# Scaling behind the SwiGLU's output products instead of ahead of them, in a fused encoder block on one Trainium2 core

## The chip, the core and the metric

The kernel runs on one core of one Trainium2 chip. The core has a matrix engine (TensorE, PE in the profile, with its weight loads as PEld), a vector engine (DVE), a scalar engine (ACT), GpSimd (POOL, hardly used here), and a sync engine (SP) whose queue issues the loads and stores. The metric is the device time of one execution in microseconds, as the median of three runs.

## What is computed

One encoder layer on 1024 tokens of 1024 channels in fp32: a half-weighted SwiGLU feed-forward (FFN1), a token mixer (retention with four heads beside a multi-scale pooling branch, both gated), a second half-weighted SwiGLU (FFN2), and a last norm. What bears on the change:

```python
D_MODEL = 1024; SEQ = 1024; D_FF = 2816; FFN_RES_WEIGHT = 0.5

def rmsnorm(x, g):
    y = x * lax.rsqrt(jnp.mean(x * x, axis=-1, keepdims=True) + NORM_EPS)
    return y * g

def swiglu_ffn(x, w_in, w_out):
    gate, up = jnp.split(x @ w_in, 2, axis=-1)
    return (jax.nn.silu(gate) * up) @ w_out

h = h + FFN_RES_WEIGHT * swiglu_ffn(rmsnorm(h, norm_ffn1), ffn1_w_in, ffn1_w_out)
...
h = h + merged @ w_out
h = h + FFN_RES_WEIGHT * swiglu_ffn(rmsnorm(h, norm_ffn2), ffn2_w_in, ffn2_w_out)
return rmsnorm(h, norm_final)
```

The norm's factor of a token is one number for each token. In the kernel it is not applied to the input of the first product but to its results: `(x g) @ w_in` is computed on unnormalised rows, and gate and up are multiplied by the factor afterwards. `silu(r·gate) · (r·up) @ w_out` equals `r · (silu(r·gate) · up) @ w_out`, since r belongs to the token.

## The kernel before

Activations lie with channels on the partitions and tokens along the free dimension, so that the factor of all tokens is a row, spread over 128 partitions into one 128x1024 tile `rb`. Each fp32 product is made as three products of rounded parts: `split` (L153 to L155) copies a value's rounded part on ACT (`hi`) and subtracts it on DVE (`lo`, L155); `mm3` (L172 to L176) issues the three matmuls on lines 174, 175 and 176. Large products are Strassen products of 512x512 blocks.

The order of the work comes from two places. `Flow` (L57 to L87) runs a chain of steps, each a pair of a preparation and a body: preparations (loads, sums, splits of weights) are issued four steps (`LOOK`) ahead of the bodies (the matmuls and their evacuations). Work that isn't urgent goes into a queue by `flow.add`, and one or two items of it are issued behind each body (`flow.rate`); `flow.until` issues such items until a condition holds. The framework then orders the instructions of each engine when it builds the program, with what stands under `soon()` (high priority) ahead of the rest. Every engine runs its instructions in that order. Tiles come from pools with fixed numbers of buffers: `mv` 28, `t4` 9, `raw` 4, `wt` 5, `tl` 4, `c2` 8 (128x512), and PSUM banks.

`ffn_in` (L699 to L769) makes the 22 groups of 128 gate channels and 128 up channels, each as a gate tile and an up tile of 128x1024. Its groups run in pairs (`pairs_of_both`, with `strassen`, L421, and `common`, L527 to L583, which shares the products of two groups in a common bank `x` that L569 and L580 evacuate). `evac` (L713 to L722) brings each 512-wide quarter of gate or up out of PSUM: where the factor is there and the quarter comes straight from one bank, L718 multiplies it on the way; otherwise it is copied or added, and a multiplication with the factor (L722) is queued. `end` queues the Silu (L728), two 512-wide products gate x up (L731), and for every second group the sums that the output stage's Strassen operands need (L744, L745, L749, L754), which are stored to DRAM (`R`, `T`, `B`, `T4`). In FFN1 the products begin before the factor is known; the groups finished by then wait with their multiplications. Names with `a_` and `n1` are FFN1's, those with `c_` and `n3` FFN2's.

`ffn_out` (L801 to L987) runs the seven Strassen products p1 to p7 over 11 steps `k` each, p1 alternating with p6, then p2 with p7, then p5, p3, p4. Its accumulators `acc` are eight 128x1024 tiles which are loaded with the residual (`res`: x, or h2 from DRAM) at `k == 6` of p1 (L829 to L832). As each product's banks end, `onto` (L891 to L896) adds half of the bank to a quarter (L894), and `after1` (L898 to L908) adds p1's halved bank, kept as `h`, to three quarters (L902, L906). When a quarter is complete it goes to `sink` through the queue: in FFN1 the next norm's quarters and a store, in FFN2 the last norm's sums of squares. In FFN2 the last product p4 is made with its operands exchanged (`near`, `far`), so that half of the tokens come out with tokens on the partitions: `split_scaled` (L157 to L159) halves the operand there, and class `Last` (L1667 to L1757) turns the accumulators for these tokens with transposes (`turned`, L1695 to L1707), finishes the rows (`finish`, L1719 to L1733), and makes the other half's norm (`end`, `fin0sum` at L223, L1754). Names with `b` (bacc, bp1a) are FFN1's output stage, those with `d` (dacc, dp4m, dL22a) FFN2's.

Of the kernel before, what the change touches and what calls it, by code (L numbers as in the profile page):

```python
# [17 lines left out]
P = 128  # L18
S = 1024
# [71 lines left out]
def block_kernel(ctx: ExitStack, tc, x, x_tok, vecs, f1_in, f1_out, w_in, w_v, pool_w, w_ret, w_pool, w_o,  # L91
# [16 lines left out]
    def mv(name):  # L108
        return sb.tile([P, 2, H], F32R, tag="mv", bufs=N_MV, name=name)
# [10 lines left out]
    def tl(name):  # L120
        return sb.tile([P, S], F32, tag="tl", bufs=N_TL, name=name)
# [4 lines left out]
    def c2(name):  # L126
        return sb.tile([P, H], F32, tag="c2", bufs=N_C2, name=name)
# [8 lines left out]
    def load(dst, src):  # L136
        nc.sync.dma_start(dst, src)
# [4 lines left out]
    def half(t, j):  # L142
        return t[:, j * H : (j + 1) * H]
# [9 lines left out]
    def split(hi, lo, src):  # L153
        copy(hi, src)
        tt(lo, src, hi.bitcast(F32), SUB)  # L155
# [5 lines left out]
    def operand(src, name):  # L161
        m = mv(name)
        split(m[:, 0], m[:, 1], src)
        return m
# [534 lines left out]
    def ffn_in(nx, w, ops, name, start=None):  # L699

        R, T, B, T4 = ops
        hid = {}

        def group(g):
            gate_up = {}

            def dest(which):
                tile, j = which
                if tile not in gate_up:
                    gate_up[tile] = (tl if start and g == 0 else t4)(f"{name}{'gu'[tile]}{g}")  # L710
                return half(gate_up[tile], j)

            def evac(which, in0, in1):  # L713
                j, dst = which[1], dest(which)
                if in1 is not None:
                    tt(dst, in0, in1, ADD)
                elif nx.rb is not None:
                    tt(dst, in0, half(nx.rb, j), MUL)  # L718
                    return
                else:  # L720
                    copy(dst, in0)
                flow.add(lambda: tt(dst, dst, half(nx.rms(), j), MUL))  # L722

            def end():
                gate, up = gate_up[0], gate_up[1]

                def swish():
                    act(gate, gate, AF.Silu)  # L728

                def times(j):  # L730
                    tt(half(up, j), half(gate, j), half(up, j), MUL)  # L731

                flow.add(swish, lambda: times(0), lambda: times(1))
                hid[g] = up
                k = g % FH
                if g < FH:
                    return
                lo, hi, e = hid.pop(k), up, {}
                R11, R12, R21, R22 = half(lo, 0), half(lo, 1), half(hi, 0), half(hi, 1)

                def w1():

                    e["n"], e["m"] = gate, c2(f"{name}m{k}")
                    tt(half(e["n"], 0), R12, R11, SUB)  # L744
                    tt(half(e["n"], 1), R22, R12, SUB)  # L745
                    load(B[k], e["n"])

                def w2():
                    tt(R12, R22, half(e["n"], 0), SUB)  # L749
                    load(R[k], lo)  # L750
                    load(T[k], hi)

                def w3():
                    tt(e["m"], R21, R12, SUB)  # L754
                    load(T4[k], e["m"])
                    done.add(k)

                flow.add(w1, w2, w3)

            if start and g == 0:  # L760
                return plain_group(nx, start, f"{name}{g}_", evac, end)
            return lambda shared: strassen(nx, w[g, 0], w[g, 1], f"{name}{g}_", evac, end, shared=shared, dest=dest)

        done = ops_done.setdefault(name, set())
        order = [g for k in range(FH) for g in (k, k + FH)]
        if start:

            return chain(group(0), pairs_of_both(nx, (group(g) for g in order[1:]), BY_OPERAND, 3))
        return pairs_of_both(nx, (group(g) for g in order), BY_OPERAND, 2)  # L769
# [28 lines left out]
    ops_done = {}  # L798


    def ffn_out(ops, ready, w, res, name, sink, end, last=None):  # L801

        R, T, B, T4 = ops
        t, acc = {}, {}
        S1, S2, S3 = {}, {}, {}

        def kept(store, n, k):
            if k % 2 == 0:  # L810
# [3 lines left out]
        def both(key, k, src):  # L814

            if k % 2 == 0:
                t[key] = (tl if key[0] != "L" else raw)(f"{name}{key}{k}")
                n = min(2, FH - k)
                for z in range(n):
                    load(half(t[key], z), src(k + z))  # L820
            return half(t[key], k % 2)

        def p1(k):
            flow.until(lambda: k in ready)
            r = tl(f"{name}r{k}")
            load(r, R[k])
            ra = raw(f"{name}ra{k}")
            load(ra, w[k, :, :S])
            if k == 6:  # L829
                for mt in range(KT):  # L830
                    acc[mt] = t4(f"{name}acc{mt}")
                    load(acc[mt], res[mt])  # L832
            t["x"] = half(ra, 0), half(ra, 1), both("L22a", k, lambda z: w[z, :, 2 * H : 3 * H])
            t["r"] = r
            return half(ra, 0), half(r, 0)
# [7 lines left out]
            return s2, half(t["r"], 1)  # L843

        def p2(k):
            r = tl(f"{name}q{k}")
            load(half(r, 0), T[k][:, :H])
            load(half(r, 1), B[k][:, H:])
            t["r"] = r
            L12, s2 = both("L12", k, lambda z: w[z, :, 3 * H :]), half(S2[k // 2], k % 2)  # L850

            tt(s2, L12, s2, SUB)
            return L12, half(r, 0)

        def p7(k):
            return half(S3[k // 2], k % 2), half(t["r"], 1)

        def p5(k):
            return half(S1[k // 2], k % 2), both("T1", k, lambda z: B[z][:, :H])

        def p3(k):
            return half(S2[k // 2], k % 2), both("R22", k, lambda z: T[z][:, H:])

        def p4(k):
            return both("L22", k, lambda z: w[z, :, 2 * H : 3 * H]), both("T4", k, lambda z: T4[z])

        bk = {}
# [20 lines left out]
        def quarter(mt, j):  # L888
            return half(acc[mt], j)

        def onto(mt, j, where, i, last=True):  # L891
            q = quarter(mt, j)
            with soon():
                stt(q, bk[where, i], 0.5, q, MUL, ADD)  # L894
            if last:
                flow.add(lambda: sink(mt, slice(j * H, (j + 1) * H), acc[mt]))  # L896

        def after1(i):  # L898
            h = c2(f"{name}p1{i}")
            with soon():  # L900
                act(h, bk["a", i], AF.Copy, scale=0.5)
                tt(quarter(i, 1), quarter(i, 1), h, ADD)  # L902

            def rest():
                for j in (1, 0):
                    tt(quarter(i + 4, j), quarter(i + 4, j), h, ADD)  # L906

            flow.add(rest)  # L908

        def after6(i):  # L910
            onto(i, 1, "b", i, False)

        def after2(i):
            onto(i, 0, "a", i)

        def after7(i):
            onto(i + 4, 1, "b", i, False)
            if last:

                onto(i + 4, 0, "b", i, False)  # L920
                if i == 3:
                    flow.add(*last.turned(acc))

        def after5(i):
            onto(i + 4, 1, "a", i)

        def after3(i):
            onto(i, 1, "a", i)
            if i == 3:
                end(0)  # L930

        def after4(i):
            onto(i + 4, 0, "b", i)
            if i == 3:
                end(1)

# [93 lines left out]
    def ffn1():  # L1030
        for n, step in enumerate(ffn_in(first, f1_in, ops1, "a", lead)):
            flow.rate = 1 if n < 40 else 2
            yield step
        yield from ffn_out(ops1, ops_done["a"], f1_out, x, "b", mix.quarter, end1)

    mix = Next("n2", V_MIX, h1)

# [727 lines left out]
    flow.run(chain(ffn1(), projections(), retention(), merge(), second(),  # L1765
                   ffn_out(ops2, ops_done.setdefault("c", set()), f2_out, h2, "d", fin.quarter, fin.end, fin)))
    flow.some(-1)


# [84 lines left out]
```

## Time and profile before

| | us |
|---|---|
| median of 3 runs | 2161.77 (2161.57 to 2161.9) |
| the profiled execution's own time | 2165.61 |
| span of that execution | 2163.8 |
| FFN1 input stage | 13 to 430 |
| FFN1 output stage | 430 to 675, the mixer's norm behind it |
| projections, retention, merge | 675 to 1540 |
| FFN2 input stage | 1540 to 1940 |
| FFN2 output stage | 1940 to 2125 |
| last products and final norm | 2125 to 2163.8 |

The profile is of one execution, whose own time is 3.8 us above the median. A row of a group of instructions reads: line, engine, operation, output <- inputs, count, durations in ns (least/median/most), first and last start, shapes. A row of the timeline reads: start, duration, engine, line, operation, and in brackets the idle time before it with what ended it. A row of the waits reads: engine, instruction, what it waited for, us in total, times, longest. Shown durations of instructions that follow each other on one engine overlap, so that a group's cost is its starts' distance, not its duration.

### The profile page before, as it was taken

How to read it: one execution, taken by the hardware profiler on the slowest of the kernel's cores; microseconds unless marked ns; L12 is line 12 of the kernel's file. 1: busy time of each engine (PE TensorE's matmuls, PEld its weight loads, DVE VectorE, ACT ScalarE, POOL GpSimd, SP SyncE). 2: the span in 40 equal slices, each digit the busy share in tenths (PEclk: the TensorE clock that was granted, in tenths of full speed). 3: DMA queues.
4: the chain of work that ended last, by engine and by line, in shares of the span. 5: the costliest groups of instructions: out<-in, count | busy, mean ns of one | idle time of the engine just before them, and what ended most of it. 6: DMA issues, size and time to landing. Idle time of an engine off the chain costs nothing.

```text
span 2163.8 us, 29697 instructions
## 1 busy us (share of the span) xinstructions
PE 2148.3 (99%) x10668; PEld 1816.2 (84%) x10668; DVE 1869.9 (86%) x3300; ACT 1088.1 (50%) x2047; POOL 0.2 (0%) x4
## 2 busy tenths in 40 slices
PE   9999999999999999999999999999999999999998
PEld 7888888888888888888888898888888888888887
DVE  8799899998778798899767877899999989999784
ACT  8544444545656444444426754446644444455463
POOL 0000000000000000000000000000000000000000
PEclk9999999999999999999999999999999999999999
DMA  7232323496323333333485567624132332359532
GB/s 255 75 118 99 115 93 124 159 337 211 127 93 98 117 127 108 115 110 116 154 268 192 166 227 255 220 92 161 64 120 100 106 104 93 117 183 336 177 122 78
DMA packets 117828, 320.92 MB, mean 148 GB/s; under 512 B 12976, under 2 KB 17200, under 8 KB 117680
## 3 DMA queue, kind: packets, MB, share of 16 engines
q1 hardware_dynamic: 117104, 317.97, 43.3%
q8 instruction: 83, 1.36, 0.3%
q10 hardware_dynamic: 576, 1.05, 0.1%
q14 instruction: 65, 0.53, 0.1%
HBM read 228.27 MB, written 90.70 MB: 147 GB/s over the span
## 4 chain that ended last, share of the span: by engine, by line
PE 89%; DVE 8%; DMA 1%; issue 1%; ACT 1%; SPq 0%; DVEq 0%; ACTq 0%
PE c_b L174 2%; PE c_b L176 2%; PE c_b L175 2%; PE c_e L176 2%; PE a_b L176 2%; PE a_b L174 2%; PE a_b L175 2%; PE c_e L175 2%; PE c_e L174 2%; PE a_e L176 1%; PE bp6b L176 1%; PE bp6b L175 1%; PE bp6b L174 1%; PE a_e L174 1%; PE a_e L175 1%; PE c_a L175 1%
## 5 line engine op out<-in xcount | busy, mean ns | idle before, releaser
L175 PE MATMUL c_b<-n3T,c_wS 128*128 128x512 f32 x176 | 68.5, 389 | 0.0
L176 PE MATMUL c_b<-n3T,c_wS 128*128 128x512 f32 x176 | 68.5, 389 | 0.0
L174 PE MATMUL c_b<-n3T,c_wS 128*128 128x512 f32 x176 | 68.3, 390 | 0.0
L174 PE MATMUL a_b<-n1T,a_wS 128*128 128x512 f32 x168 | 65.4, 389 | 0.0
L176 PE MATMUL a_b<-n1T,a_wS 128*128 128x512 f32 x168 | 65.4, 389 | 0.0
L175 PE MATMUL a_b<-n1T,a_wS 128*128 128x512 f32 x168 | 65.4, 389 | 0.0
L176 PE MATMUL a_a<-n1R,a_wL 128*128 128x512 f32 x120 | 47.0, 393 | 0.8 <-DVE a_wL L155 0.8
L175 PE MATMUL a_a<-n1R,a_wL 128*128 128x512 f32 x120 | 47.2, 393 | 0.0
L174 PE MATMUL a_a<-n1R,a_wL 128*128 128x512 f32 x120 | 47.1, 393 | 0.0
L175 PE MATMUL c_a<-n3R,c_wL 128*128 128x512 f32 x112 | 43.8, 391 | 0.0
L176 PE MATMUL c_a<-n3R,c_wL 128*128 128x512 f32 x112 | 43.7, 390 | 0.0
L174 PE MATMUL c_a<-n3R,c_wL 128*128 128x512 f32 x112 | 43.6, 389 | 0.0
L176 PEld LDWEIGHTS c_b<-n3T,c_wS 128*128 128x128 f32 x176 | 33.0, 188 | 6.9
L174 PEld LDWEIGHTS c_b<-n3T,c_wS 128*128 128x128 f32 x176 | 33.1, 188 | 6.8
L175 PEld LDWEIGHTS c_b<-n3T,c_wS 128*128 128x128 f32 x176 | 33.1, 188 | 6.8
L174 PEld LDWEIGHTS a_b<-n1T,a_wS 128*128 128x128 f32 x168 | 31.5, 188 | 6.7 <-ACT a_v L477 0.2
L175 PEld LDWEIGHTS a_b<-n1T,a_wS 128*128 128x128 f32 x168 | 31.5, 188 | 6.6
L176 PEld LDWEIGHTS a_b<-n1T,a_wS 128*128 128x128 f32 x168 | 31.5, 188 | 6.5
L176 PE MATMUL c_e<-n3T,c_wS 128*128 128x512 f32 x88 | 35.1, 399 | 0.5 <-DVE c_wS L155 0.4
L174 PE MATMUL c_e<-n3T,c_wS 128*128 128x512 f32 x88 | 34.4, 391 | 0.0
L176 PE MATMUL c_e<-n3T,c_wL 128*128 128x512 f32 x88 | 34.4, 391 | 0.0
L175 PE MATMUL c_e<-n3T,c_wL 128*128 128x512 f32 x88 | 34.4, 391 | 0.0
(3058 smaller groups left out, 8071.0 us busy)
## 6 DMA issues: line engine op xcount, KB each, us to landing
c_ra<-in_f_in SPq DMA_DIRECT2D x22, 512.0 KB, 3.6
c_rb<-in_f_in SPq DMA_DIRECT2D x22, 512.0 KB, 4.2
a_ra<-in_f_in SPq DMA_DIRECT2D x21, 512.0 KB, 3.6
a_rb<-in_f_in SPq DMA_DIRECT2D x21, 512.0 KB, 4.3
t<-au SPq DMA_DIRECT2D x11, 512.0 KB, 2.6
b<-ag SPq DMA_DIRECT2D x11, 512.0 KB, 2.7
r<-au SPq DMA_DIRECT2D x11, 512.0 KB, 3.6
br<-r SPq DMA_DIRECT2D x11, 512.0 KB, 6.1
```

The source lines that it names most:

```text
L174: mm(dst, w[0], m[0], start=start, stop=False, skip_group_check=True)
L175: mm(dst, w[0], m[1], start=False, stop=False, skip_group_check=True)
L176: mm(dst, w[1], m[0], start=False, stop=stop, skip_group_check=True)
```

## The change

In `ffn_in` only gate is multiplied by the factor; up stays unscaled. Where both quarters of a gate tile still lack the factor, one 128x1024 multiplication applies it, just ahead of the Silu; the product gate x up is one 128x1024 instruction in place of two of 512.

In `ffn_out` the missing factor is applied to the results. `rows()` makes a tile 0.5 x factor at `k == 6` of p1, where the accumulators were loaded with the residuals; the accumulators now begin empty. `onto` is a plain addition of a bank. When a quarter is complete, `done` queues its scaling by the tile, the addition of its residual, and the sink. The residuals are loaded late, in 128x512 halves, at the ninth step of p2, p5 and p3 into `raw` tiles, and at the ninth step of p4 (FFN1, `tl`) or p7 (FFN2, `c2`). p1's banks are copied out whole (`p1s`) and kept until the end of p7. In `near` the operand is multiplied by the tile and then split, where it was split and halved at once.

```diff
@@ ffn_in
             def evac(which, in0, in1):
-                j, dst = which[1], dest(which)
+                tile, j = which
+                dst, rms = dest(which), nx.rb
                 if in1 is not None:
                     tt(dst, in0, in1, ADD)
-                elif nx.rb is not None:
-                    tt(dst, in0, half(nx.rb, j), MUL)
+                elif not tile and rms is not None:
+                    tt(dst, in0, half(rms, j), MUL)
                     return
                 else:
                     copy(dst, in0)
-                flow.add(lambda: tt(dst, dst, half(nx.rms(), j), MUL))
+                if not tile:
+                    later.append(j)
...
-                def swish():
+                def scale():
+                    if len(later) == 2:
+                        tt(gate, gate, nx.rms(), MUL)
+                    else:
+                        for j in later:
+                            tt(half(gate, j), half(gate, j), half(nx.rms(), j), MUL)
                     act(gate, gate, AF.Silu)
 
-                def times(j):
-                    tt(half(up, j), half(gate, j), half(up, j), MUL)
-
-                flow.add(swish, lambda: times(0), lambda: times(1))
+                flow.add(scale, lambda: tt(up, gate, up, MUL))
@@ ffn_out
+        def rows():
+            t["rb"] = sb.tile([P, S], F32, tag="mv", bufs=N_MV, name=f"{name}rb")
+            act(t["rb"], nx.rms(), AF.Copy, scale=0.5)
+
+        def residual(mts, j, tile, two=2):
+            for n in range(0, 4, two):
+                r = tile(f"{name}res{mts[n]}{j}")
+                for z, mt in enumerate(mts[n : n + two]):
+                    load(half(r, z), res[mt][:, j * H : (j + 1) * H])
+                    old[mt, j] = half(r, z)
...
             if k == 6:
+                rows()
                 for mt in range(KT):
                     acc[mt] = t4(f"{name}acc{mt}")
-                    load(acc[mt], res[mt])
...
         def p2(k):
+            if k == FH - 3:
+                residual(TOP, 0, raw)
...
         def p7(k):
+            if last and k == FH - 3:
+                residual(LOW, 0, c2, 1)
...
         def p5(k):
+            if k == FH - 3:
+                residual(LOW, 1, raw)
...
         def p3(k):
+            if k == FH - 3:
+                residual(TOP, 1, raw)
...
         def p4(k):
+            if not last and k == FH - 3:
+                residual(LOW, 0, tl)
...
-        def onto(mt, j, where, i, last=True):
+        def onto(mt, j, where, i, before=None):
             q = quarter(mt, j)
             with soon():
-                stt(q, bk[where, i], 0.5, q, MUL, ADD)
+                tt(q, bk[where, i], q if before is None else before, ADD)
+
+        def scale(q, src, j):
+            tt(q, src, half(t["rb"], j), MUL)
+
+        def done(mt, j, to=sink, scaled=False):
+            q = quarter(mt, j)
+
+            def end():
+                if not scaled:
+                    scale(q, q, j)
+                tt(q, q, old.pop((mt, j)), ADD)
+                if to:
+                    to(mt, slice(j * H, (j + 1) * H), acc[mt])
+
+            flow.add(end)
+
+        def after1(i):
+            p1s[i] = c2(f"{name}p1{i}")
+            with soon():
+                copy(p1s[i], bk["a", i])
+
+        def after6(i):
+            onto(i, 1, "b", i, p1s[i])
+
+        def after2(i):
+            with soon():
+                scale(quarter(i, 0), bk["a", i], 0)
+            done(i, 0, scaled=True)
+
+        def after7(i):
+            onto(i + 4, 1, "b", i, p1s[i])
             if last:
-                flow.add(lambda: sink(mt, slice(j * H, (j + 1) * H), acc[mt]))
-
-        def after1(i):
-            h = c2(f"{name}p1{i}")
-            with soon():
-                act(h, bk["a", i], AF.Copy, scale=0.5)
-                tt(quarter(i, 1), quarter(i, 1), h, ADD)
-
-            def rest():
-                for j in (1, 0):
-                    tt(quarter(i + 4, j), quarter(i + 4, j), h, ADD)
-
-            flow.add(rest)
...
+                onto(i + 4, 0, "b", i, p1s[i])
+                done(i + 4, 0, None)
                 if i == 3:
                     flow.add(*last.turned(acc))
+            else:
+                copy(quarter(i + 4, 0), p1s[i])
 
         def after5(i):
             onto(i + 4, 1, "a", i)
+            done(i + 4, 1)
...
         def near(k):
             def prep():
                 l, r = p4(k)
+                scale(r, r, 0)
                 L[k], X[k] = operand(l, f"{name}p4w{k}"), mv(f"{name}p4m{k}")
-                split_scaled(X[k][:, 0], X[k][:, 1], r, 0.5)
+                split(X[k][:, 0], X[k][:, 1], r)
```

`after3` and `after4` end with `done` as `after5` does.

More of the change, by code (lines that the diff above doesn't have):

```diff
@@ L711, in dest @@
                 return half(gate_up[tile], j)
+            later = []
             def evac(which, in0, in1):
-                j, dst = which[1], dest(which)
+                tile, j = which
+                dst, rms = dest(which), nx.rb
                 if in1 is not None:
                     tt(dst, in0, in1, ADD)
-                elif nx.rb is not None:
-                    tt(dst, in0, half(nx.rb, j), MUL)
+                elif not tile and rms is not None:
+                    tt(dst, in0, half(rms, j), MUL)
                     return
@@ L798, in block_kernel, with ffn_out @@
     ops_done = {}
-    def ffn_out(ops, ready, w, res, name, sink, end, last=None):
+    def ffn_out(nx, ops, ready, w, res, name, sink, end, last=None):
         R, T, B, T4 = ops
-        t, acc = {}, {}
+        t, acc, old, p1s = {}, {}, {}, {}
         S1, S2, S3 = {}, {}, {}
+        def rows():
[7 more added lines that the diff above has]
+                    old[mt, j] = half(r, z)
+        TOP, LOW = range(4), range(4, 8)
         def kept(store, n, k):
@@ L889, in quarter @@
             return half(acc[mt], j)
-        def onto(mt, j, where, i, last=True):
+        def onto(mt, j, where, i, before=None):
             q = quarter(mt, j)
             with soon():
-                stt(q, bk[where, i], 0.5, q, MUL, ADD)
-            if last:
-                flow.add(lambda: sink(mt, slice(j * H, (j + 1) * H), acc[mt]))
-        def after1(i):
-            h = c2(f"{name}p1{i}")
-            with soon():
-                act(h, bk["a", i], AF.Copy, scale=0.5)
-                tt(quarter(i, 1), quarter(i, 1), h, ADD)
-            def rest():
-                for j in (1, 0):
-                    tt(quarter(i + 4, j), quarter(i + 4, j), h, ADD)
-            flow.add(rest)
[L910 to L920, printed above, removed]
+                tt(q, bk[where, i], q if before is None else before, ADD)
[22 more added lines that the diff above has]
+            onto(i + 4, 1, "b", i, p1s[i])
+            if last:
+                onto(i + 4, 0, "b", i, p1s[i])
+                done(i + 4, 0, None)
                 if i == 3:
                     flow.add(*last.turned(acc))
+            else:
+                copy(quarter(i + 4, 0), p1s[i])
         def after5(i):
             onto(i + 4, 1, "a", i)
+            done(i + 4, 1)
         def after3(i):
             onto(i, 1, "a", i)
+            done(i, 1)
             if i == 3:
@@ L933, in after4 @@
             onto(i + 4, 0, "b", i)
+            done(i + 4, 0)
             if i == 3:
@@ L1033, in ffn1 @@
             yield step
-        yield from ffn_out(ops1, ops_done["a"], f1_out, x, "b", mix.quarter, end1)
+        yield from ffn_out(first, ops1, ops_done["a"], f1_out, x, "b", mix.quarter, end1)
     mix = Next("n2", V_MIX, h1)
@@ L1765, in block_kernel @@
     flow.run(chain(ffn1(), projections(), retention(), merge(), second(),
-                   ffn_out(ops2, ops_done.setdefault("c", set()), f2_out, h2, "d", fin.quarter, fin.end, fin)))
+                   ffn_out(ffn2, ops2, ops_done.setdefault("c", set()), f2_out, h2, "d", fin.quarter, fin.end, fin)))
     flow.some(-1)
```

## The prediction

> **What bounds the kernel now.** I read the page's busy times and its chain of waits first, then the busy times by stage, then what TensorE waits for, then the single places.
>
> ```profile
> span 2163.8 us, 29697 instructions
> PE 2148.3 (99%) x10668; PEld 1816.2 (84%) x10668; DVE 1869.9 (86%) x3300; ACT 1088.1 (50%) x2047; POOL 0.2 (0%) x4
> PE 89%; DVE 8%; DMA 1%; issue 1%; ACT 1%; SPq 0%; DVEq 0%; ACTq 0%
> ```
>
> TensorE is busy for 99% of the span and carries 89% of the chain; VectorE has the next 8%. The change leaves every product, so TensorE's own work is a floor, and only what TensorE loses beside it can be won. The stages (start and end, length, then busy time and count of PE, weight loads, DVE, ACT, POOL, then granted clock and DMA share) say where:
>
> ```profile
> 13.00:430.00 417.00, 414.08 (x2104) 351.63 (x2103) 382.10 (x693) 217.22 (x401) 0.00 (x0) 1.00 0.36 124
> 430.00:675.00 245.00, 245.00 (x1090) 202.92 (x1089) 202.44 (x338) 131.70 (x234) 0.00 (x0) 1.00 0.54 182
> ...
> 1540.00:1940.00 400.00, 398.15 (x2113) 342.19 (x2113) 373.39 (x691) 196.43 (x367) 0.00 (x0) 1.00 0.33 111
> 1940.00:2125.00 185.00, 185.00 (x833) 153.29 (x832) 150.01 (x248) 92.75 (x168) 0.00 (x0) 1.00 0.59 198
> ```
>
> The first and third rows are the two SwiGLU input stages: DVE is busy for 92% and 93% of them, and TensorE is idle for 2.92 and 1.85 us. The second and fourth are the output stages (the second with the norm behind it): TensorE never idles, and DVE has 42.6 and 35.0 us free. The waits name the engine:
>
> ```profile
> PE c_x L174 <- DVE cg L569: 1.3, 1, 1.3
> PE a_x L174 <- DVE ag L569: 0.9, 2, 0.7
> PE a_e L176 <- DVE a_wS L155: 0.9, 2, 0.5
> PE a_a L176 <- DVE a_wL L155: 0.8, 1, 0.8
> PE c_e L176 <- DVE c_wS L155: 0.4, 1, 0.4
> ```
>
> All five, 4.3 us together, stand in the input stages and end on DVE. Idle time is not all that is lost: matmuls overlap, so a short gap is hidden in their busy time.
>
> ```profile
> 334.71 0.39 PE L174 MATMUL a_e<-n1T,a_wS 128*128 128x512 f32 x1
> 334.93 0.39 PE L175 MATMUL a_e<-n1T,a_wS 128*128 128x512 f32 x1
> 335.39 0.50 PE L176 MATMUL a_e<-n1T,a_wS 128*128 128x512 f32 x1
> ```
>
> The second starts 0.22 us behind the first, the usual pitch, and the third 0.46 us behind the second. Adding up every start-to-start distance of the two input windows (2104 and 2113 matmuls) above 0.227 us for a 512-wide and 0.118 for a 256-wide one gives 8.1 and 4.3 us. This 12.4 us is what the change can win there; the same count finds 0.3 to 0.5 us in either output stage.
>
> **The largest spot.** Its windows, in the columns of the stages above, and the matmul that waited:
>
> ```profile
> 86.06:128.67 42.61, 41.58 (x192) 33.62 (x191) 42.61 (x80) 19.42 (x34) 0.00 (x0) 1.00 0.38 136
> 125.00:128.00 3.00, 2.02 (x9) 1.39 (x10) 3.00 (x8) 1.36 (x5) 0.00 (x0) 1.00 0.00 0
> 128.30:131.70 3.40, 3.40 (x14) 3.01 (x13) 2.75 (x6) 1.03 (x2) 0.00 (x0) 0.50 0.00 0
> 127.54 0.50 PE L176 MATMUL a_a<-n1R,a_wL 128*128 128x512 f32 x1 [0.77 <-DVE a_wL L155]
> ```
>
> When the norm's factor arrives at 86 us, multiplies for the groups already finished crowd onto DVE, which then has not one idle instant in 42.61 us. TensorE thins out at the end of it (2.02 us busy of 3.00), and then runs at half clock for 3.40 us, which costs 1.7 us. With the gaps from 121 to 132 us this spot is 4.15 of FFN1's 8.1 us.
>
> [...]
>
> **Part 1, the input stages.** What is removed, and the prices:
>
> ```profile
> L722 DVE TENSOR_TENSOR au<-au,n1rb x44: 681/685/689, 86.7 to 438.1; 128x512 f32<-128x512 f32 x44
> L722 DVE TENSOR_TENSOR cu<-cu,n3rb x44: 678/683/692, 1561.9 to 1947.9; 128x512 f32<-128x512 f32 x44
> L722 DVE TENSOR_TENSOR cg<-cg,n3rb x38: 677/683/689, 1560.1 to 1939.5; 128x512 f32<-128x512 f32 x38
> L722 DVE TENSOR_TENSOR ag<-ag,n1rb x37: 678/683/693, 86.1 to 429.7; 128x512 f32<-128x512 f32 x37
> L731 DVE TENSOR_TENSOR au<-ag,au x44: 682/685/692, 90.9 to 441.1; 128x512 f32<-128x512 f32 x44
> L731 DVE TENSOR_TENSOR cu<-cg,cu x44: 678/685/692, 1568.5 to 1950.9; 128x512 f32<-128x512 f32 x44
> ...
> 754.43 1.22 DVE L1060 TENSOR_TENSOR cos<-cos,n2rb 128x1024 f32<-128x1024 f32 x1
> 755.57 1.22 DVE L1060 TENSOR_TENSOR sin<-sin,n2rb 128x1024 f32<-128x1024 f32 x1
> 756.70 0.42 DVE L569 TENSOR_TENSOR q0A<-q0x,k0A 128x256 f32<-128x256 f32 x1
> ```
>
> Before there are 163 late multiplies and 88 products, 251 in all, 512 wide. In the built order of the changed program they become 13 half multiplies, 31 whole gate multiplies and 44 whole products (the 13 multiplies that read a bank directly stay). A 512-wide one shows 0.68 us, but its successor starts 0.60 us later (1934.64 to 1935.24, quoted below); a 1024-wide one takes 1.13 by the starts above. So 251 x 0.60 = 151 us becomes 13 x 0.60 + 75 x 1.13 = 93 us: 58 us less, 29 per FFN, about 2.6 us per pair of groups. What that buys is found by summing the same pitches along the changed order, from the same starting point:
>
> - In the rush the last first-level weights come 36.0 instead of 41.2 us behind the factor. The 5.2 us gained is more than the about 2.5 us lost in gaps there (4.15 − 1.7), so gaps and half clock should both go.
> - In steady state one pair's DVE work falls from 32.7 to 30.6 us and the weights L155 that c_e waits for come 0.9 us earlier, where 0.24 us is short.
> - At the end of each input stage DVE waited for a load:
>
> ```profile
> 1927.68 0.69 DVE L840 TENSOR_TENSOR ds<-dra,dL22a 128x512 f32<-128x512 f32 x1 [1.99 <-DMA dL22a<-in_f_out]
> ...
> 1934.64 0.68 DVE L155 TENSOR_TENSOR dp1m<-dr,dp1m 128x512 fp32r<-128x512 f32 x1
> 1935.24 0.42 DVE L569 TENSOR_TENSOR cg<-c_x,cg 128x256 f32<-128x256 f32 x1
> ```
>
> L840 is first in line for a load whose buffer came free with an earlier DVE subtraction (L452), and L569 follows 13 instructions behind. In the changed order the same 13 lie between, but that subtraction comes 2.1 us earlier: L569 starts at 1933.1, where TensorE wants its result at 1934.3. The 1.45 us lost there, and 0.85 us at FFN1's end, go.
>
> I take 7.0 of 8.1 and 3.5 of 4.3 us, keeping 1.9 for gaps not traced one by one: **−10.5**, between 0 and −12.4.
>
> **Part 2, the output stages.** One row each of the old accumulation, the residual loads, and the stretch in which FFN2's residuals land:
>
> ```profile
> L894 DVE SCALAR_TENSOR_TENSOR dacc<-dp6b,dacc x12: 679/680/687, 2000.4 to 2064.3; 128x512 f32<-128x512 f32 x12
> L137 SPq DMA_DIRECT2D dacc<-h x8: 320/402/747, 1923.4 to 1962.3; - x8
> 1950.00:2000.00 50.00, 50.00 (x222) 41.44 (x221) 47.47 (x79) 26.46 (x49) 0.00 (x0) 1.00 0.95 337
> ```
>
> The 72 accumulating instructions (48 L894, 8 L902, 16 L906) become 40 additions, 43 scalings (11 of them on the last operand) and 32 residual additions: 43 more, 43 x 0.60 = +26 us, 13 per FFN, against 42.6 and 35.0 us of free DVE. Scaling straight out of a bank is priced like L894, which reads one too. ACT exchanges 8 scaled copies for 14 plain or scaled ones, at 50% load. The burst matters more than the mean: around the end of p7, 24 DVE operations stand where 12 stood, 7.2 us more. Operands are made four steps of 2.7 us ahead, and by the changed order p5's fourth weights are ready at 2066.7 against 2069.9, its seventh at 2074.5 against 2078: nothing lost. Without that cover it would cost 7.2 us per FFN.
>
> The residuals (4 MB per FFN, the same bytes) leave the stretch where the 16 DMA engines are 95% busy and are issued on the same SP queue in 256 KB pieces during the ninth steps of p2, p5, p3 and p7 or p4. The new wait is the residual addition on DVE: if its load is late, the splits L155 of coming operands stand behind it, and TensorE behind these. L840's 1.99 us is the nearest price of one such wait; with four batches per FFN that is 0 to 16 us over both FFNs, less three steps of prepared operands (8 us) in front of each. I take 0.
>
> **Part 3, the tail.**
>
> ```profile
> 2124.12 2.48 DVE L894 SCALAR_TENSOR_TENSOR dacc<-dp5a,dacc 128x512 f32<-128x512 f32 x4
> 2126.52 3.07 DVE L260 TENSOR_TENSOR n4ssq<-n4ssq,n4q 128x512 f32<-128x512 f32 x4
> 2129.22 0.39 PE L176 MATMUL n4s<-dp4w,dp4m 128*128 128x512 f32 x1
> 2129.73 1.02 PE L223 MATMUL fin0sum<-cst,n4ssq 128*128 128x1 f32 x8
> ```
>
> Behind p3's last products, 8 more DVE instructions (4 scalings, 4 residual additions) stand ahead of the sums of squares, 4.8 us. The built order puts fin0sum 25 products later (25 x 0.227 = 5.7 us), so it loses 0 to 0.5 us where 0.28 is lost now (0.51 between the two starts above, less 0.23). The last operand ends near 2135.5, needed at 2139.2. What follows the last matmul is unchanged in the built order. I take **+0.3**, between −0.3 and +4.8 (if nothing covers the eight).
>
> **Sum.** −10.5 + 0 + 0.3 = −10.2; I round to −10. Against the profiled execution's own 2165.61 us (span 2163.8 and 1.8 around it) that is 2155.6; it ran 3.8 us above the median, so from 2161.77 the forecast is **2152 us**.
>
> **Rivals.**
>
> *Nothing gained, 2162.* The freed DVE time turns into DVE idling because another wait stands close behind, on ACT's half of a split or on a weight load. For it: L840's wait is a DMA's. Against it: the five waits end on DVE, and in the rush DVE never idled.
>
> *Half the gain given back, 2156.* The residual additions or the tail's eight operations are not covered: +4 us on the sum, by the bounds of parts 2 and 3.
>
> *The half clock stays, 2154.* If the clock drops by its own timing, 1.7 us of the gain is absent: 2152 + 1.7. For it: TensorE's single idle gap was only 0.77 us. Against it: the drop follows directly on the thinnest stretch.
>
> *Slower, about 2170.* The change puts 75 operations of 1.13 us in place of 0.60 us ones on an in-order engine. They can delay the 66 evacuations of the bank that two groups share (L569 and L580, 18 + 15 each). The margin is short:
>
> ```profile
> 1874.62 0.41 DVE L569 TENSOR_TENSOR cg<-c_x,cg 128x256 f32<-128x256 f32 x1
> ...
> 1875.30 0.28 PE L174 MATMUL c_x<-n3R21y,c_ws 128*128 128x256 f32 x1
> ```
>
> L569 ends at 1875.03 and TensorE needs it at 1875.30. Each evacuation caught loses up to 0.53 us (1.13 − 0.60): 66 make 35 us, half of them 17.5, so 2170. It cancels the gain from 19 of 66 on. Against it: in the changed order the nearest instructions ahead of L569 are 512 wide or narrower, and it comes 0.8 us earlier.
>
> **Chances and range.** Forecast (2149.4 to 2155) 0.50, half clock stays 0.10, half given back 0.12, nothing gained 0.14, slower 0.14. About 0.2%, 4.3 us, is what a measurement of this kernel can tell from no change. Below 2157.4 lie the first two and most of the third: faster 0.70. Nothing gained and the rest: same 0.16; slower 0.14. The range runs from 2149 (all 12.4 us won) to 2162, which leaves out the slower case and a little of the unchanged one; the forecast's own is 2149 to 2155.
>
> **What would show it.** DVE in the first input window at about 353 us instead of 382; in the two output windows some 13 us more. No half clock near 130 us; no wait of TensorE on L569 near 425 and 1934 us. Wrong if these waits go and new ones of TensorE on ACT or DMA add up to as much, if idle appears between 500 and 670 or 2050 and 2125 us behind residual additions, or if fin0sum stalls by more than 1 us.

## The result and the profile after

The changed kernel takes 2173.34 us in the median of 4 runs (2172.57 to 2173.7), the kernel before 2161.84 (2161.57 to 2162.15): 11.5 us or 0.53% slower, ratio 1.0053 with a 95% interval from 1.0037 to 1.0069. The forecast was 10 us the other way. The page after, its span, busy times and chain:

```profile
span 2171.9 us, 29623 instructions
PE 2149.8 (99%) x10668; PEld 1816.7 (84%) x10668; DVE 1839.5 (85%) x3180; ACT 1093.9 (50%) x2053; POOL 0.2 (0%) x4
PE 90%; DVE 6%; ACT 1%; issue 1%; DMA 1%; SPq 0%; DVEq 0%; ACTq 0%
```

VectorE (DVE) has 30 us less to do (1869.9 before), yet the span is 8 us longer. The stages after, in the same windows as before, with the projections between the two feed-forwards added (start and end, length, busy time and count of PE, PEld, DVE, ACT, POOL, granted clock, DMA share, GB/s):

```profile
13.00:430.00 417.00, 414.27 (x2118) 352.77 (x2117) 358.31 (x621) 217.81 (x401) 0.00 (x0) 1.00 0.37 127
430.00:675.00 245.00, 245.00 (x1090) 203.11 (x1089) 206.53 (x338) 131.67 (x233) 0.00 (x0) 1.00 0.54 176
675.00:1175.00 500.00, 494.28 (x2371) 416.80 (x2370) 419.76 (x706) 219.13 (x404) 0.00 (x0) 0.99 0.42 140
...
1540.00:1940.00 400.00, 397.32 (x2088) 340.53 (x2087) 346.90 (x614) 195.12 (x362) 0.00 (x0) 1.00 0.31 107
1940.00:2125.00 185.00, 185.00 (x850) 153.65 (x849) 155.07 (x254) 92.41 (x168) 0.00 (x0) 1.00 0.62 202
```

DVE fell from 382 to 358 us in the first input stage and from 373 to 347 us in the second, but TensorE still idles there (2.73 and 2.68 us), and 5.72 us of idle time appear in the projections, a stage that the diff doesn't touch. What TensorE waits for, after:

```profile
PE p0e L174 <- ACT p0wS L154: 5.7, 1, 5.7
PE a_b L174 <- ACT a_wS L154: 1.3, 1, 1.3
PE c_b L174 <- ACT c_wS L154: 1.3, 1, 1.3
...
PE a_b L176 <- DVE a_wS L155: 1.2, 3, 0.5
PE c_b L176 <- DVE c_wS L155: 1.1, 3, 0.5
```

All five waits of before are off the list. In their place stand one long wait at the start of the projections and two kinds of wait in the input stages, one product (`c_b`, `a_b`) further on than the old ones (`c_e`, `a_e`).

The table counts TensorE's losses as the prediction did, start to start above the pitch, by stage (a stage begins with its first matmul). Two profiles of the kernel before stand in it, the second from a later run; the three experiments are described below.

| us lost | before | before, again | changed | spaced queue (e4) | input stages alone, spaced (e8) | e9 |
|---|---|---|---|---|---|---|
| FFN1 input | 8.1 | 8.2 | 5.0 | 2.7 | 2.1 | 2.2 |
| projections | 0.6 | 0.6 | 8.5 | 8.1 | 0.6 | 2.7 |
| FFN2 input | 4.5 | 3.4 | 6.7 | 2.1 | 2.8 | 2.3 |
| FFN2 output and tail | 0.9 | 0.8 | 1.5 | 1.3 | 0.8 | 1.4 |
| elsewhere | 7.0 | 6.7 | 7.3 | 6.1 | 6.8 | 6.5 |
| sum | 21.2 | 19.7 | 28.9 | 20.4 | 13.1 | 15.1 |
| span | 2163.8 | 2161.8 | 2171.9 | 2163.0 | 2155.9 | 2156.9 |

From the second profile of before to the changed kernel: −3.2 in FFN1's input, +7.9 in the projections, +3.3 in FFN2's input, +1.3 in the rest, +9.2 in sum, against 10.1 us of span. The gain expected in the input stages came in part, and two new losses of 8 and 3 us came with it.

A stage's loss differs between profiles of the same code. By the same count FFN1's unchanged input stage loses 6.2 and 6.9 us in e2 and e10, against 8.1 and 8.2 in the two columns of before; the changed one loses 7.1 in e3 against 5.0 here; the changed FFN2 input loses 5.2 in e7 against 6.7 here. Most of each difference is one stretch of half clock, 1.6 to 1.7 us, that came or did not come (shown below).

**The loss at the projections.** The wait, and DVE's rows just ahead of it, from the changed kernel's timeline (start, duration, engine, line, operation, idle time before it and its end in brackets):

```profile
682.01 0.39 PE L176 MATMUL p0a<-n2R,p0wL 128*128 128x512 f32 x1
688.12 0.80 PE L174 MATMUL p0e<-n2T,p0wS 128*128 128x512 f32 x1 [5.72 <-ACT p0wS L154]
688.71 0.63 PE L175 MATMUL p0e<-n2T,p0wS 128*128 128x512 f32 x1
689.14 0.63 PE L176 MATMUL p0e<-n2T,p0wS 128*128 128x512 f32 x1
```

```profile
682.31 0.68 DVE L1131 TENSOR_TENSOR t0B<-t0B,n2rb 128x512 f32<-128x512 f32 x1
682.91 0.68 DVE L1131 TENSOR_TENSOR t1B<-t1B,n2rb 128x512 f32<-128x512 f32 x1
683.51 0.68 DVE L1131 TENSOR_TENSOR t0A<-t0A,n2rb 128x512 f32<-128x512 f32 x1
...
685.05 0.68 DVE L435 TENSOR_TENSOR p0S<-p0rb 128x512 f32<-128x512 f32 x1
685.99 0.68 DVE L448 TENSOR_TENSOR p0rb<-p0ra,p0rb 128x512 f32<-128x512 f32 x1
```

The split of `p0wS` on ACT waits for `p0rb` from DVE, and DVE comes to that subtraction (L448) only at 685.99, because multiplications with the mixer's norm factor (n2rb) stand ahead of it. In the kernel before the same subtraction came 3.7 us ahead of TensorE's first use:

```profile
679.59 0.69 DVE L435 TENSOR_TENSOR p0S<-p0rb 128x512 f32<-128x512 f32 x1
680.19 0.69 DVE L1077 TENSOR_TENSOR t0B<-t0e,t0v 128x512 f32<-128x512 f32 x1
...
681.72 0.69 DVE L448 TENSOR_TENSOR p0rb<-p0ra,p0rb 128x512 f32<-128x512 f32 x1
```

```profile
685.41 0.39 PE L174 MATMUL p0e<-n2T,p0wS 128*128 128x512 f32 x1
```

What crowded DVE in the changed kernel lies ahead of that. Below are the stretch from p3's end to the projections in both kernels, and the new instructions from 600 to 690 us in the changed one (count, busy time, mean ns, idle time).

Before:

```profile
611.00:690.00 79.00, 79.00 (x357) 65.31 (x356) 72.78 (x134) 52.05 (x94) 0.00 (x0) 1.00 0.33 110
```

Changed:

```profile
611.00:690.00 79.00, 73.28 (x327) 60.09 (x327) 76.32 (x138) 48.38 (x88) 0.00 (x0) 0.97 0.33 110
```

```profile
L927 DVE TENSOR_TENSOR bacc<-bacc,brb 128x512 f32<-128x512 f32 x8 | 5.3, 678 | 0.0
L935 DVE TENSOR_TENSOR bacc<-bacc,bres 128x512 f32<-128x512 f32 x8 | 5.3, 678 | 0.0
```

DVE had 6.2 us free in these 79 us. The 16 new instructions, at their pitch of 0.60 us, are 9.6 us. From p3's last addition to `p0S` DVE runs 130 instructions in the changed kernel's trace and 110 in that of before, and idles for 2.7 us there instead of 6.1. The 20 more are the 16 new ones and four of the mixer's own: the evacuations of `t0B` and `t1B` and their multiplications with n2rb. These four stood behind `p0S` before (`t0B` at 680.19 above) and stand ahead of it now.

**The clock behind it.** Two stretches in which TensorE lacked work, each followed by the stretch after it, and a third with the same lack in FFN1, all of the changed kernel:

```profile
682.00:688.10 6.10, 0.40 (x2) 0.00 (x0) 6.10 (x13) 4.90 (x8) 0.00 (x0) 0.83 0.43 172
688.10:692.60 4.50, 4.48 (x11) 3.39 (x12) 4.50 (x11) 4.16 (x8) 0.00 (x0) 0.50 0.31 120
1695.50:1699.60 4.10, 2.26 (x10) 1.23 (x9) 4.07 (x8) 1.91 (x4) 0.00 (x0) 1.00 0.68 263
1699.60:1703.00 3.40, 3.40 (x10) 2.67 (x9) 3.34 (x6) 1.86 (x4) 0.00 (x0) 0.53 0.40 125
...
251.00:255.00 4.00, 2.16 (x9) 1.18 (x8) 3.96 (x8) 1.76 (x4) 0.00 (x0) 1.00 0.70 273
```

The wait of 5.72 us is followed by 4.5 us at half clock, which shows in the four rows of matmuls above as starts 0.43 us apart instead of 0.227 us: twelve distances that cost 2.3 us more. A gap of 1.29 us near 1697, in a stretch with TensorE busy for 55% (2.26 of 4.10 us), is followed by half clock too, and the same gap near 252, in a stretch with TensorE busy for 54% (2.16 of 4.00 us), is not.

Shorter stretches around these gaps don't tell the two apart either. Below are 3.41 us near 252 and near 1697 in the changed kernel, then such a stretch near 252 and the one behind it in e3, an experiment described below, all in the same columns:

```profile
251.30:254.71 3.41, 1.57 (x7) 0.67 (x6) 3.38 (x6) 1.62 (x3) 0.00 (x0) 1.00 0.74 288
1695.50:1698.91 3.41, 1.57 (x7) 0.67 (x6) 3.38 (x7) 1.37 (x3) 0.00 (x0) 1.00 0.81 316
```

```profile
250.86:254.28 3.42, 1.58 (x7) 0.68 (x6) 3.38 (x7) 1.36 (x3) 0.00 (x0) 1.00 0.82 317
254.28:257.69 3.41, 3.41 (x9) 2.64 (x10) 3.41 (x7) 2.03 (x4) 0.00 (x0) 0.50 0.18 43
```

TensorE is busy for 1.57 us in both stretches of the changed kernel and for 1.58 us in that of e3. Behind the first the clock stays full, behind the other two it is half; what decides between them was not shown. The gap near 252 was followed by half clock in e3 and not in the changed kernel, e1 and e7; the gap near 1697 in the changed kernel, e2 and e3 and not in e7; and the half clock near 128 of the kernel before came again in e6 and not in e2 and e10, which have the same FFN1.

### The profile page after: what moved, and what is told of

Same layout as the page of the kernel before. It is cut to its first block, busy times and chain, and to the rows that moved or that the text cites. A ratio compares the mean times of both kernels' runs of the same rounds, so it can differ in the third digit from the quotient of the medians.

```text
span 2171.9 us, 29623 instructions
## 1 busy us (share of the span) xinstructions
PE 2149.8 (99%) x10668; PEld 1816.7 (84%) x10668; DVE 1839.5 (85%) x3180; ACT 1093.9 (50%) x2053; POOL 0.2 (0%) x4
## 4 chain that ended last, share of the span: by engine, by line
PE 90%; DVE 6%; ACT 1%; issue 1%; DMA 1%; SPq 0%; DVEq 0%; ACTq 0%
PE c_b L176 2%; PE a_b L176 2%; PE c_b L175 2%; PE c_b L174 2%; PE a_b L174 2%; PE a_b L175 2%; PE c_e L175 2%; PE c_e L174 2%; PE a_e L175 2%; PE c_e L176 2%; PE a_e L176 2%; PE a_e L174 2%; PE bp6b L176 1%; PE bp6b L174 1%; PE bp6b L175 1%; PE a_a L176 1%
## 5 line engine op out<-in xcount | busy, mean ns | idle before, releaser
L154 ACT CAST a_wS<-a_S 128x512 fp32r<-128x512 f32 x45 | 27.1, 620 | 16.4 <-DVE a_S L435 8.5
L176 PE MATMUL c_e<-n3T,c_wL 128*128 128x512 f32 x88 | 34.4, 391 | 0.0
```

Source lines behind the costliest of these rows:

```text
L176: mm(dst, w[1], m[0], start=False, stop=stop, skip_group_check=True)
```

## The experiments

Each ran beside the kernel before on the same chip, and the ratios are to those runs (its medians there were 2163.1 to 2163.5 us, single runs 2160.7 to 2165.9). The experiments ran on three chips, so times of two kernels are compared by what each takes over the kernel before beside it.

**e1 and e2: one feed-forward changed at a time.** The old functions are kept beside the new ones.

```diff
 # e1
-ffn_in(ffn2, f2_in, ops2, "c")
+ffn_in_old(ffn2, f2_in, ops2, "c")
-ffn_out(ffn2, ops2, ...)
+ffn_out_old(ops2, ...)
 # e2: the same for FFN1 instead
```

> Only FFN1 (input and output stage) is changed, FFN2 stays as before. If the time goes at the end of FFN1, where 16 more VectorE instructions stand ahead of the projections' first weights, most of the 11.5 us is here: about 2170 us, with TensorE's wait of 5.9 us for p0wS near 682 us and the half clock behind it as in the changed kernel. If both feed-forwards cost alike, about 2167.5 us. If FFN1 gains as forecast and FFN2 loses, below 2162 us.

> Only FFN2 is changed. If the end of FFN1 is the cause, the rest by the stages of the two profiles is +2.2 us in the input stage and +0.6 us in the output stage and tail: about 2164.6 us, and no wait for p0wS. If both feed-forwards cost alike, about 2167.5 us.

e1 took 2169.12 us, ratio 1.0027 (1.0017 to 1.0036), with the wait for p0wS:

```profile
PE p0e L174 <- ACT p0wS L154: 5.7, 1, 5.7
PE a_b L176 <- DVE a_wS L155: 1.4, 4, 0.5
PE a_b L174 <- ACT a_wS L154: 1.3, 1, 1.3
```

e2 took 2166.55 us, ratio 1.0013 (1.0003 to 1.0022), without it. Two thirds of the loss belong to FFN1, by the wait at its end; the rest is FFN2's, whose input stage loses 6.7 us here as in the changed kernel. That both cost alike is excluded by the traces more than by the times.

**e3 and e7: eight instructions fewer at the end of FFN1.** e3 leaves out scaling and residual of p4's quarters, e7 those of p3's, some 30 us earlier.

```diff
         def after4(i):           # e7: after3
             onto(i + 4, 0, "b", i)
-            done(i + 4, 0)
+            if last:
+                done(i + 4, 0)
+            else:
+                flow.add(lambda: sink(i + 4, slice(0, H), acc[i + 4]))
```

> The changed kernel without the scaling and the residual addition of p4's four quarters in FFN1 (8 VectorE instructions of 0.60 us left out, their loads stay). If VectorE's load at the end of FFN1 is the cause, the wait for p0wS falls from 5.9 to about 1.1 us and the half clock behind it goes: 2173.3 - 4.8 - 2.1 = about 2166.4 us. If the wait comes from something else (a load, a buffer, TensorE arriving earlier because the input stage gained), these 8 instructions change little: above 2171 us.

> The changed kernel without the scaling and the residual addition of p3's four quarters in FFN1 (8 VectorE instructions, 30 us ahead of the ones left out before). If VectorE is booked out from p3's end to the projections, it is all the same which 8 are missing: wait for p0wS about 1.4 us. If only what stands behind p4's last matmul counts, the wait stays at 5.9 us.

e3 took 2167.15 us, ratio 1.0017 (1.0007 to 1.0026), e7 2164.67 in one run. What TensorE waits for in e3 and the window around it, then the same two for e7:

```profile
PE p0e L174 <- ACT p0wS L154: 1.2, 1, 1.2
```

```profile
683.00:690.00 7.00, 5.64 (x24) 4.05 (x23) 7.00 (x16) 6.42 (x13) 0.00 (x0) 1.00 0.46 181
```

```profile
PE p0e L174 <- ACT p0wS L154: 1.2, 1, 1.2
```

```profile
683.00:690.00 7.00, 6.54 (x28) 5.10 (x28) 6.99 (x16) 5.66 (x14) 0.00 (x0) 1.00 0.22 87
```

Eight instructions, 4.8 us of DVE, take 4.5 us off the wait, the half clock goes (1.00 in both windows), and the projections lose 2.2 us instead of 8.5. It is the same whichever eight: DVE is nearly booked out from p3's end on, and what counts for these 4.5 us is how many instructions stand ahead of the projections' first weights, not their place or a late load.

**e4: the queue spaced as before.** The changed kernel issues fewer items per group: no multiplication of `up`, one product instead of two. Empty items fill the places.

```diff
                 if not tile:
                     later.append(j)
+                flow.add(lambda: None)
...
-                flow.add(scale, lambda: tt(up, gate, up, MUL))
+                flow.add(scale, lambda: None, lambda: tt(up, gate, up, MUL))
```

> The changed kernel with empty items in the queue where it has fewer than before, so that the gate multiplications, products and sums are issued in as many steps as before. If the shorter queue bunches them ahead of the weights' sums, the new waits of the input stages go (2.2 us near 252 us, 2.2 us and a half clock of 1.6 us near 1696 us, some 0.3 us for each of 9 pairs): 2173.3 - 8.7 = about 2165 us. If the instructions themselves, 1024 wide, make these waits, it stays at 2172 to 2174 us.

It took 2165.66 us, ratio 1.0009 (1.0 to 1.0019): 2.5 us above the kernel before, where the changed kernel stood 11.5 us above it, with the same number of instructions on every engine (its span is 8.9 us shorter). First the changed kernel's DVE around FFN2's fourth pair of groups, where the wait at 1697 arises:

```profile
1690.10 1.23 DVE L739 TENSOR_TENSOR cu<-cg,cu 128x1024 f32<-128x1024 f32 x1 [1.02 <-ACT cg L737]
1691.24 0.69 DVE L155 TENSOR_TENSOR c_wS<-c_rb,c_wS 128x512 fp32r<-128x512 f32 x1
1691.85 0.42 DVE L569 TENSOR_TENSOR cg<-c_x,cg 128x256 f32<-128x256 f32 x1
1692.18 0.68 DVE L750 TENSOR_TENSOR cg<-cu 128x512 f32<-128x512 f32 x1
...
1695.52 0.68 DVE L760 TENSOR_TENSOR cm<-cu,cu 128x512 f32<-128x512 f32 x1
1696.11 0.68 DVE L435 TENSOR_TENSOR c_S<-c_S,c_ra 128x512 f32<-128x512 f32 x1
```

The weights' sum L435, for which ACT's split and TensorE wait, stands behind the product (L739) and the four sums of the output stage (L750 to L760), and DVE even waits 1.02 us for the Silu ahead of all that. Then the same with the spaced queue:

```profile
1675.65 0.68 DVE L448 TENSOR_TENSOR c_rb<-c_ra,c_rb 128x512 f32<-128x512 f32 x1
1676.25 0.69 DVE L435 TENSOR_TENSOR c_S<-c_S,c_ra 128x512 f32<-128x512 f32 x1
...
1679.92 1.21 DVE L734 TENSOR_TENSOR cg<-cg,n3rb 128x1024 f32<-128x1024 f32 x1
```

The first sum (L435, directly behind L448) is now made ahead of the gate's multiplication, and the input stages leave TensorE almost no gap:

```profile
13.00:430.00 417.00, 416.62 (x2128) 354.92 (x2127) 362.13 (x627) 218.36 (x403) 0.00 (x0) 1.00 0.38 128
1540.00:1940.00 400.00, 399.82 (x2125) 344.10 (x2124) 350.49 (x619) 197.65 (x367) 0.00 (x0) 1.00 0.33 112
```

So the long instructions aren't the cause; the number of queued items is, since nothing else differs. That the shorter queue runs dry sooner and hands its work to the program ahead of weights that are needed first is read from `Flow` and fits the order shown; the queue itself was not traced. The wait for p0wS stays at 5.7 us, although TensorE came to it 3 us earlier than in the changed kernel (679 us against 682): DVE moves with TensorE, and the gain of the input stage is not what makes the wait.

**e8: the input stages alone.** New, spaced input stages, old output stages. This kernel leaves out the factor on up altogether, so it is a measure and not a complete kernel.

```diff
-ffn_out(first, ops1, ops_done["a"], ...)
+ffn_out_old(ops1, ops_done["a"], ...)      # and the same for FFN2
```

> Only the input stages are changed, with the spaced queue; the output stages are those of before (the factor on up is left out). The input stages lose 2.7 and 2.1 us as in the spaced kernel, and there is no wait for p0wS: TensorE loses 20.4 - 7.5 - 0.4 = about 12.5 us in all, and the time is 8 us below the spaced kernel's. If the gain of the input stages is given back behind FFN1 whatever the output stage does, a wait for p0wS of some us remains.

It took 2157.82 us in one run beside 2163.48 for before, and its span is 7.1 us shorter than the spaced kernel's; TensorE loses 13.1 us, and no wait for p0wS is left. This is what the input stages gain where nothing is paid behind them: 6 us of span against before's second profile.

**e6: the kernel before, once more.**

> The kernel before once more, for a second profile. If its first profile, 3.8 us above the median, lost more than its usual run in the first FFN1 stretch (half clock and gaps from 121 to 132 us), this one loses some 4 us less in the input stage of FFN1 than 8.1 us. If the stages vary little, 8.1 us again.

It took 2163.62 us in one run. The expectation that the first profile had an untypical FFN1 fell: 8.2 us again in its input stage. What differed is FFN2's wait on L569 near 1933 us, 0.5 us lost instead of 1.45, where DVE waits 1.03 instead of 1.99 us for a load (L840). Why the first profiled execution stood 3.8 us above the median stays open beyond that 1 us; its 2165.61 us lie within the single runs of the kernel before named above.

**e5 and e9: fewer instructions at FFN1's end.** In FFN1 the partial sums are scaled and given their residual ahead of the last bank, while DVE has time; at a product's end the last bank is scaled and added (2 instructions a quarter instead of 3; 1 before). All of it stands on e4's queue. In e5 p5's banks were scaled in place although p3 goes on summing in them, so that p5's share is scaled twice there; e9 uses a tile for them.

```diff
+        def ahead(mts, j):
+            def pre(mt):
+                q = quarter(mt, j)
+                scale(q, q, j)
+                tt(q, q, old.pop((mt, j)), ADD)
+            flow.add(*(lambda mt=mt: pre(mt) for mt in mts))
+
+        def close(mt, j, where, i):
+            q, b = quarter(mt, j), bk[where, i]
+            to = c2(f"{name}last{mt}{j}") if mt >= 4 and j else b      # e5: to = b
+            with soon():
+                scale(to, b, j)
+                tt(q, to, q, ADD)
+            flow.add(lambda: sink(mt, slice(j * H, (j + 1) * H), acc[mt]))
...
         # FFN1: residual(LOW, 0, c2, 1) and ahead(LOW, 0) at p5 k = 0 and 3, (LOW, 1) at 4 and 7,
         # (TOP, 1) at p3 k = 0 and 4; after5, after3 and after4 call close
```

> Spaced queue as in the run before, and in FFN1 the partial sums are scaled and given their residual during p5 and p3; at the ends of p5, p3 and p4 only the last bank is scaled in place and added (8 VectorE instructions in place of 12; 4 before). If the number of VectorE instructions at the end of FFN1 sets the wait for p0wS, it is at most the 1.4 us of the run without p4's scalings, and no half clock follows: the projections lose 2.5 us instead of 8.1, about 5.5 us below the spaced kernel: 2160 us, below the kernel before. If the place of the last additions, which stay 8, decides instead, it stays near 2165.7 us.

> As the early version, but p5's banks are scaled into a tile of their own, since p3 goes on summing in them. TensorE's wait for those banks (1.5 us) goes, the rest stays: loses about 2.4 (FFN1 input) + 2.5 (projections) + 2.5 (FFN2 input) + 8 elsewhere = 15.5 us against 19.7 of the kernel before: about 4 us below it, 2159.5 us. If the end of FFN1 only moves its wait, within 1 us of the kernel before.

e5 took 2161.71 us, ratio 0.9992 (0.9983 to 1.0002): a wait of 1.5 us of `bp5a`, TensorE's next product into the banks in use, on DVE's scaling (L895) appeared near 576 us, and the projections lost 2.5 us. e9 took 2160.36 us against 2163.23, ratio 0.9987 (0.9978 to 0.9996), the only complete kernel that is clear of the one before on the fast side. Its waits:

```profile
PE p0e L174 <- ACT p0wS L154: 1.2, 1, 1.2
...
PE p0e L176 <- DVE p0wS L155: 0.5, 1, 0.5
```

With 118 instead of 130 instructions between p3's last addition and `p0S`, the wait is where e3 and e7 had it, with 123. So five instructions fewer took nothing more off, and the 1.2 us that remain are not explained by the count alone. The 8 beyond the 110 of before are 4 of the new scalings and the mixer's four that moved ahead of `p0S`; e9 loses 2.0 us more than e8, by the table all of it in the projections. Whether the mixer's four make this wait, no run tests.

**e10: FFN1 as before, FFN2 changed with the spaced queue.**

> FFN1 as before, FFN2 changed with the spaced queue. FFN2's input stage loses 2.1 to 2.8 instead of 3.4 to 4.5 us, its output stage and tail 0.5 us more: about 1 us below the kernel before. If the long instructions and the late residuals cost by themselves, above it.

It took 2162.86 us against 2163.23, ratio 0.9998 (0.9989 to 1.0007): no difference that the runs can tell, with 2.8 us lost in FFN2's input and 1.6 us in its output and tail. The gain of the second feed-forward is about as large as its price.

## Why the prediction was wrong, step by step

- *What bounds, and what can be won.* Right in kind: the losses of the input stages come from DVE and can be won. By the table 12.6 us stood there (11.6 in the second profile); e4 and e8 leave 4.8 and 4.9. But 1.7 us of the 8.1 were half clock, which two profiles of the same FFN1 do not have (e2 and e10, 6.2 and 6.9 us lost): a part that depends on the execution was counted as a fixed loss.
- *Part 1, the waits named.* The five waits went in the changed kernel, the half clock near 130 us too; DVE's busy time came to 358 us where 353 was forecast. The wait on L569 near 1934 went in part by luck: with the same input stage as e4, e5 waits there for 0.9 us, behind a load that DVE waits 2.04 us for. The failed step is "What that buys is found by summing the same pitches along the changed order": the sums ran to the weights of `c_e`, which waited before, and not to those of `c_b`, which stand next to them and came to wait in their place. Nor did the prediction ask what the smaller number of queued items does to the order. −10.5 forecast; −3.2 in FFN1 and +3.3 in FFN2 measured, 1.6 of the latter being half clock (e4: −5.5 and −1.3; all against the second profile).
- *Part 2, the output stages.* The failed step that cost most: "43 x 0.60 = +26 us, 13 per FFN, against 42.6 and 35.0 us of free DVE". The free time was a mean over 245 us. In the 79 us from p3's end it was 6.2 us, against 9.6 us of new work, and the stage's last wait stands in the next stage, behind work that queues for DVE: 5.7 us of wait and 2.3 us of half clock. The 43 additional instructions are all there (3300 − 163 + 43 = 3180, the page's count), yet the two output windows show 4.1 and 5.1 us more, not some 13 each: the first holds 338 DVE instructions as before, so about as many others left it, at its front (the input stage ended 3 us earlier) or past 675 us. The burst at p7's end was worked out and held (0.0 us lost in FFN1's output stage; 0.9 in FFN2's, where it was 0.3 to 0.5); the burst at p3's and p4's end was not worked out at all for FFN1. The residual loads cost nothing, as forecast: no instruction of DVE waits for one.
- *Part 3, the tail.* +0.3 forecast, +0.2 by the count.
- *The clock.* The rival took the half clock as 1.7 us that might stay by its own timing. It went from its place with the gap and came at two others, 2.3 and 1.6 us, each behind a new wait. The gap alone does not decide, though: two profiles with the old FFN1 (e2 and e10) have the gap without the half clock. That the clock drops by a timing of its own was not shown.
- *The rivals.* "Slower", at about 2170 us, comes near the measured 2173 by luck, for it had the wrong mechanism: the 1024-wide instructions do not hold up L569, for e4 has all of them and no such wait above 0.2 us. "Half the gain given back" named the right instructions, the uncovered scalings and residual additions, with the wrong place and half the price. The signal named for it, idle behind residual additions, came 12 us outside the window it was given, at 682 us.

## What to carry to other kernels

Work that is moved from a full engine in one stage to the same engine in another must be set against that engine's free time between the last result of the old stage and the first need of the next, not against the stage's mean: 79 us with 6 us free decided here, in a stage with 42 us free.

Where work goes out through a queue that is drained at a fixed rate, taking items away moves everything behind them forward; look at what that puts ahead of the operand that is needed next, and sum up to every consumer, not only to those that waited before.

## What the runs showed of the hardware

Two TensorE waits cost more than their length: behind 5.72 us of idle time the matmuls started 0.43 us apart instead of 0.227 for 4.5 us, 2.3 us more, and behind a gap of 1.29 us in a thin stretch (TensorE busy for 2.26 of 4.10 us) the clock fell near 1697 us, 1.6 us more; behind the same gap near 252 us (2.16 of 4.00 us busy) it did not. With the wait cut to 1.2 us the half clock did not come in e3, e7 and e9 (granted clock 1.00 from 683 to 690 us, in e9 from 672 to 690 us). Eight 512-wide DVE instructions less shortened the wait of another engine by 4.5 us, close to their 0.60 us each, at p3's end as at p4's.
